# One level of Strassen's recursion in the first product of a squared-ReLU MLP, with the weight sums on POOL

## Chip, cores and metric

The kernel runs on one core of a Trainium2 chip. The metric is the device time of one execution in microseconds; before the change it was 2098.53 us, the median of three runs (2090.01 to 2098.53). In the profile PE is TensorE's matmuls, PEld its weight loads, DVE VectorE, ACT ScalarE, POOL GpSimd and SP the engine that issues the loads.

## What is computed

A trunk of two layers works on 640 tokens of 1024 features: 128 tokens of a prompt and 512 of a sample. Each layer has a token mixer (spatial gating in layer 0, RWKV-7 in layer 1) and an MLP; both are residual and behind an RMS norm that is modulated by a condition (adaLN). Only the MLP's line is touched:

```python
h = _rmsnorm(x, P['norm2_g'][l]) * (1 + sc2) + sh2
x = x + g2 * (jnp.square(jax.nn.relu(h @ P['mlp_w1'][l])) @ P['mlp_w2'][l])
```

`mlp_w1` is 1024 x 4096 and `mlp_w2` 4096 x 1024, in float32.

## The kernel before

Activations lie feature-major: a tile is 128 features by 640 tokens, and the 1024 features are 8 tiles. Products in float32 precision are made from float32r operands: each operand is split in a high and a low part (ScalarE casts, VectorE subtracts), and three products are summed, high by high, high by low and low by high. So one output tile of an MLP product takes 8 k-chunks x 3 parts x 2 token ranges = 48 matmuls, of 256 and of 384 columns in turn (`mmh`, L112 to L114; the halves HS are tokens 0 to 255 and 256 to 639, since a PSUM bank holds 512 float32 numbers of a partition). The sum of an output tile lies in one of three PSUM buffers (`fmps`).

`mlp` (L406 to L453) goes in four blocks (fb). In each block the first product gives 8 of the 32 hidden tiles, and the second product adds their share to the 8 output tiles. `fm` (L230) drives both: for each output tile it takes the 512 KB weight tile that has been loaded and split one group ahead (L82 to L89: a load on SP, a cast of 128x1024 on ScalarE at L88, a subtraction on VectorE at L89), runs the 48 matmuls and calls the evacuation. For the first product that is `ev1`: ReLU on ScalarE (L433), the square on VectorE (L435), and the split (L100, L101). For the second it is the residual sum on VectorE (L283). In the first block the first tiles are taken token half by token half (three tiles in layer 0, two in layer 1), since the second half's normalized activations are made (`enter`, L417) while PE works on the first half's. In layer 0 this is also where eight steps of the last adaLN projection run (`ada_steps`, L117, called by a hook after output tiles); PE takes about 1 us for one. Layer 0 takes the half of 256 tokens first, layer 1 that of 384.

Engines run their instructions in order, and a scheduler has put each engine's in an order by priority. The MLP of layer 0 runs from about 243 to 704 us of the profiled execution, that of layer 1 from about 1635 to 2093 us.

Of the kernel before, what the change touches and what calls it, by code (L numbers as in the profile page):

```python
# [7 lines left out]
F32 = mybir.dt.float32  # L8
# [20 lines left out]
def tile_trunk(ctx: ExitStack, tc: tile.TileContext, a: dict):  # L29
# [128 lines left out]
    class Norm:  # L158
# [5 lines left out]
        def add(self, k, r=(0, T)):  # L164
            for h, (t0, t1) in enumerate(HS):
                if r[0] <= t0 and t1 <= r[1]:
                    if self.acc[h] is None:
                        self.acc[h] = self.pool.tile([P, t1 - t0], F32, tag=f"acc{h}", name="acc")
                    self.gather(h, k == 0, X[k][:, t0:t1], self.pool.tile([P, 384], F32, tag="sq", name="sq")[:, :t1 - t0])
# [8 lines left out]
        # in two steps, with room for other products while the first one's result is worked on  # L178
# [49 lines left out]
    # groups: (tiles, order) - order of token halves when a group takes them one after the other, with its feature  # L228
    # tiles inside ("k": as inputs come) or one by one ("n": so that the first half is done early)
# [47 lines left out]
    # first half's statistics while the second half's products run  # L277
# [9 lines left out]
    def sgu(wp, norm):  # L287
        with ExitStack() as es:
# [8 lines left out]
            with ExitStack() as e2:  # L297
# [18 lines left out]
                # the first products follow their inputs, tile by tile  # L316
# [61 lines left out]
            up = Pool(es, "sguu", {"ah": 8, "al": 8})  # L378
# [24 lines left out]
    MB = (4, 3, 11)  # L403
    ST = ((3, 7), (2, 4))

    def mlp(wp, norm, l, first, last, hp=None, mp=None, pre=None):  # L406
        with ExitStack() as es:
            hp = hp or Pool(es, f"mlph{l}", {"ah": 8, "al": 8})
            sp = Pool(es, f"mlps{l}", {"ah": MB[2] if l else 11, "al": MB[2] if l else 11})
            mp = mp or Pool(es, f"mlpm{l}", {"r": 2, "q": 2})  # L410
            pre = pre or [wp.get(a["w1"][l, n]) for n in range(3)]
            n0 = len(pre)
            pp = Pool(es, f"pml{l}", {"f": 3}, PSUM)
            hs = [parts(hp) for _ in range(KT)]
            o0, o1 = map(int, first[1:])

            def enter(h):  # L417
                with urgent(h != o0):
                    bc = norm.rstd(h)
                    for k in range(KT):  # L420
                        fill(hs[k], norm.apply(k, bc, l, 1, h), HS[h])

            enter(o0)
            nn = Norm(npool)
            if l == 0:
                side.append(ada_steps(wp, 1, 0, 2))
            for fb in range(4):
                ss = {}

                def ev1(n, ps, rg):  # L430
                    m = rg[1] - rg[0]
                    r = mp.tile([P, T], F32, tag="r", name="relu")[:, :m]
                    act.activation(out=r, in_=ps, func=AF.Relu)  # L433
                    q = mp.tile([P, T], F32, tag="q", name="rsq")[:, :m]
                    vec.tensor_tensor(out=q, in0=r, in1=r, op=ALU.mult)  # L435
                    if n not in ss:
                        ss[n] = parts(sp)
                    fill(ss[n], q, rg)

                fm(wp, pp, "f", list(range(8)), lambda n: a["w1"][l, fb * 8 + n], hs, ev1,  # L440
                   [(n0, first)] + [1] * (8 - n0) if fb == 0 else None,
                   {(o0, ST[l][0]): lambda: norm.stats(o1), (o0, ST[l][1]): lambda: enter(o1)} if fb == 0 else {},
# [1286 lines left out]
```

## Time and profile before

| what | value |
|---|---|
| median of three runs | 2098.53 us |
| runs | 2090.01, 2098.53, 2098.53 us |
| span of the profiled execution | 2109.0 us |
| MLP of layer 0, about | 243 to 704 us |
| MLP of layer 1, about | 1635 to 2093 us |
| HBM traffic over the span | 123 GB/s |

The profiled execution's span is the time that its rows cover, 10.5 us above the median of the runs without the profiler. Rows of a timeline give an instruction's start, its duration and, in brackets, the idle time of its engine ahead of it with what ended that. Rows of a group give the count, then the sum of the durations in us and the mean in ns, then the idle time ahead of all of them. A row of a window gives the stretch in us, then busy time and count for PE, PEld, DVE, ACT and POOL, then the granted TensorE clock (1.00 is full speed), the DMA share and GB/s.

### The profile page before, as it was taken

What the parts mean: (1) busy time and instruction counts of PE and PEld (TensorE: products, weight loads), DVE (VectorE), ACT (ScalarE), POOL (GpSimd) and SP (SyncE); (2) the same over time, 40 slices, a digit from 0 to 9 for tenths busy, and PEclk for the clock granted to TensorE, in tenths of its full rate; (3) what the DMA queues carried; (4) which work ended last, traced back from release to release, by engine and by line L of the source; (5) the groups of instructions that cost most, each with busy time, mean ns of one, the idle gap of its engine ahead of it and who ended that gap; (6) DMA issues with size and microseconds to landing.
All of it is one profiled execution on the core that took longest, in us unless ns stands there. A gap on an engine that the chain in (4) does not pass through costs nothing.

```text
span 2109.0 us, 39157 instructions
## 1 busy us (share of the span) xinstructions
PE 1991.5 (94%) x15882; PEld 1739.6 (82%) x15882; DVE 1162.9 (55%) x2308; ACT 774.5 (37%) x1737; POOL 389.3 (18%) x689
## 2 busy tenths in 40 slices
PE   6999999999999789988869999999998999999997
PEld 5777889999999678877747766767787999999996
DVE  5435643333333796766786577787658533333334
ACT  5323531312222255444524444554434522222231
POOL 0000000000000200477551465465201000000000
PEclk9999999999999889987869879998799999999998
DMA  8777352222222033554655444552242222222221
GB/s 286 265 266 233 105 184 80 71 81 70 80 71 75 36 96 121 171 151 129 186 159 175 143 131 148 166 160 80 71 130 76 67 74 75 76 74 77 73 67 51
DMA packets 124438, 254.58 MB, mean 121 GB/s; under 512 B 24417, under 2 KB 63969, under 8 KB 124129
## 3 DMA queue, kind: packets, MB, share of 16 engines
q1 hardware_dynamic: 123824, 251.62, 37.3%
q8 instruction: 125, 2.05, 0.4%
q14 instruction: 57, 0.46, 0.1%
q10 hardware_dynamic: 432, 0.46, 0.1%
HBM read 214.67 MB, written 45.22 MB: 123 GB/s over the span
## 4 chain that ended last, share of the span: by engine, by line
PE 85%; DVE 6%; POOL 3%; ACT 2%; issue 2%; DMA 1%; SPq 0%; DVEq 0%; POOLq 0%; ACTq 0%
PE fmps L114 47%; PE zps L310 6%; PE p L910 4%; PE wops L1180 3%; PE vps L751 2%; PE za L1039 2%; PE za L1026 2%; PE sy L1053 2%; PE sy L1034 1%; PE rps L114 1%; PE trps L932 1%; PE adaps L1166 1%; PE adaps L122 1%; PE sy L1036 1%; PE tps L980 1%
## 5 line engine op out<-in xcount | busy, mean ns | idle before, releaser
L114 PE MATMUL fmps<-ahi,whi 128*128 128x256 f32 (+1 forms) x2272 | 534.6, 310 | 4.9 <-ACT ahi L100 3.1
L114 PE MATMUL fmps<-alo,whi 128*128 128x256 f32 (+1 forms) x2272 | 533.8, 309 | 1.3 <-DVE alo L101 1.3
L114 PE MATMUL fmps<-ahi,wlo 128*128 128x256 f32 (+1 forms) x2272 | 533.8, 309 | 0.0
L114 PEld LDWEIGHTS fmps<-ahi,whi 128*128 128x128 f32 x2272 | 414.4, 188 | 11.0 <-ACT ahi L100 6.3
L114 PEld LDWEIGHTS fmps<-alo,whi 128*128 128x128 f32 x2272 | 415.0, 188 | 2.1 <-DVE alo L101 1.8
L114 PEld LDWEIGHTS fmps<-ahi,wlo 128*128 128x128 f32 x2272 | 415.2, 188 | 1.0 <-issue 0.8
L88 ACT CAST whi<-wraw 128x1024 fp32r<-128x1024 f32 x174 | 182.6, 1050 | 632.6 <-PE fmps L114 538.2
L89 DVE TENSOR_TENSOR wlo<-wraw,whi 128x1024 fp32r<-128x1024 f32 x174 | 214.4, 1233 | 276.2 <-ACT whi L88 276.1
L283 DVE SCALAR_TENSOR_TENSOR x<-fmps,mod,x 128x128 f32<-128x128 f32 (+2 forms) x153 | 74.5, 527 | 305.4 <-PE fmps L114 305.4
L491 POOL TENSOR_TENSOR xx<-h 128x254 f32<-128x254 f32 (+1 forms) x16 | 12.1, 754 | 721.2 <-DVE h L210 706.1
L841 POOL TENSOR_TENSOR inv<-inv 128x220 f32<-128x220 f32 (+29 forms) x217 | 100.7, 464 | 114.4 <-DVE inv L834 57.7
L910 PE MATMUL p<-W,IT 128*128 128x256 f32 x320 | 109.6, 453 | 10.0 <-DVE B L925 5.9
L843 POOL TENSOR_TENSOR inv<-inv 128x220 f32<-128x220 f32 (+29 forms) x217 | 104.5, 482 | 16.9
L1042 ACT ACTIVATE RZ<-za 64x64 f32<-64x64 f32 x320 | 58.4, 214 | 66.7 <-PE za L1039 53.9
L1060 DVE TENSOR_TENSOR RZ<-sy,PC 64x64 f32<-64x64 f32 x256 | 49.4, 219 | 60.2 <-PE sy L1054 52.5
L101 DVE TENSOR_TENSOR alo<-rsq,ahi 128x640 fp32r<-128x640 f32 (+2 forms) x69 | 53.6, 776 | 45.6 <-ACT ahi L100 45.3
L100 ACT CAST ahi<-rsq 128x640 fp32r<-128x640 f32 (+2 forms) x69 | 47.5, 689 | 82.2 <-DVE rsq L435 81.8
L910 PEld LDWEIGHTS p<-W,IT 128*128 128x128 f32 x320 | 57.9, 211 | 22.9 <-DVE B L925 6.3
L1054 PE MATMUL sy<-RZ,B 128*64 128x64 f32 x640 | 72.6, 251 | 0.6 <-ACT RZ L1042 0.6
L1026 PEld LDWEIGHTS za<-RZ,W 128*64 128x64 f32 x640 | 43.5, 154 | 33.8 <-DVE RZ L1060 9.0
L1026 PE MATMUL za<-RZ,W 128*64 128x64 f32 x640 | 62.5, 254 | 8.4 <-DVE RZ L1080 5.9
L1036 PE MATMUL sy<-RZ,W 128*64 128x64 f32 x640 | 69.1, 249 | 0.0
(289 smaller groups left out, 3428.4 us busy)
## 6 DMA issues: line engine op xcount, KB each, us to landing
wraw<-w SPq DMA_DIRECT2D x126, 512.0 KB, 3.5
wraw<-ada SPq DMA_DIRECT2D x64, 512.0 KB, 4.9
W<-dKR SPq DMA_DIRECT2D x80, 256.0 KB, 3.5
adaw<-adac SPq DMA_DIRECT2D x32, 512.0 KB, 4.4
dKR<-zero SPq DMA_DIRECT2D x32, 320.0 KB, 6.3
dKR<-KR SPq DMA_DIRECT2D x32, 320.0 KB, 4.1
dIT<-IT SPq DMA_DIRECT2D x16, 640.0 KB, 3.3
IT<-dIT SPq DMA_DIRECT2D x80, 128.0 KB, 2.9
```

The costliest lines, as they stand in the source:

```text
L88: act.copy(hi[:, :n], r[:, :n])
L89: vec.tensor_tensor(out=lo[:, :n], in0=r[:, :n], in1=hi[:, :n], op=ALU.subtract)
L114: pe.matmul(ps[:, PS0 + t0:PS0 + t1], w, x[:, t0:t1], start=start, stop=stop)
L283: vec.scalar_tensor_tensor(out=X[n][:, t0:t1], in0=ps[:, t0 - r[0]:t1 - r[0]], scalar=mod[l][:, which, n, g:g + 1], in1=X[n][:, t0:t1], op ...
L310: pe.matmul(pss[i], x[:, i * P:(i + 1) * P], w[:, kq * 512:(kq + 1) * 512], start=(k == 0 and j == 0), stop=(k == KT - 1 and j == 2))
L841: eng.tensor_tensor(out=tv, in0=LA[:, s + 1:32, s:s + 1].to_broadcast([P, n, m]), in1=LX[:, s:s + 1, c0:c1].to_broadcast([P, n, m]), op=AL ...
L843: eng.tensor_tensor(out=LX[:, s + 1:32, c0:c1], in0=LX[:, s + 1:32, c0:c1], in1=tv, op=ALU.subtract)
L910: pe.matmul(ps[:, :, 2 * e:2 * e + 2].rearrange("p h s t -> p h (s t)"), IT[:, e], W[:, :, 2 * e:2 * e + 2].rearrange("p h s t -> p h (s t ...
L1026: pe.matmul(za[a0:a0 + 64, 0], W[:, h, 3 * e], RZ[:, ti, h, c], start=True, stop=True)
L1036: pe.matmul(sy[y0:y0 + 64, h], W[:, h, 1 + e], RZ[:, ti, h, c], start=h == 0, stop=False)
L1054: pe.matmul(sy[y0:y0 + 64, h], B[:, h, 3 * e], RZ[:, ti, h, c], start=False, stop=h == 1)
L1180: pe.matmul(ps, u, v, start=start and j == 0, stop=stop and j == 2)
```

## The change

The first product of an MLP is a product of a 2 x 2 block matrix of weights (two output tiles by two halves of the 1024 input features) with a 2 x 2 block matrix of activations (the two halves of the input features by two halves of 320 tokens). A *pair* of output tiles is now made by seven products of quarters instead of eight. Each of the seven has 4 k-chunks x 3 parts = 12 matmuls of 320 columns, so a pair has 84 matmuls of 320 columns where two tiles had 96 of 256 or 384. Their operands are sums of quarters:

- **Activations**, once in a layer (`combos`): the two quarters that are used plainly are copied or left in place, four sums of quarters are made and split. For each of four j that is an add of 640 on POOL and one on VectorE (L596, high part and low part of a tile back to one number), four combinations of 320 on VectorE (L600), a cast of 1280 on ScalarE (L562) and its low part on VectorE (L563).
- **Weights**, for each pair (`Pair.make`): four sums of 128x512 on POOL (L475 to L478), in place in the raw tiles but for the first, s1, which has a ring of two slots; then splits: one of 1024 and five of 512. The weights of a product are made two steps ahead, in a ring of three; five raw tiles are loaded ahead.
- **Results** (`pair`): the seven sums go through three PSUM banks A, B and C in the order of products 2, 1, 5, 6, 3, 7, 4. Products that belong to several quarters of the result are accumulated in one bank; ScalarE copies, VectorE adds, then one instruction does ReLU and square (L607), and the split follows as before.

The first four output tiles of each layer stay plain (`first_mm`, `first_out`; L613 to L630), 14 pairs follow. The second product is as before. Its order of blocks is the same too. The adaLN steps have moved from the first tiles into the second products of blocks 1 to 3. Scratch of the norm has smaller rings (squares 3 to 2, statistics 4 to 2 and others), the raw and split pools belong to the MLP alone, and the plain tiles' scratch (`ct`) shares the ring of s1.

```diff
+    ORD = ((2, "C", 512), (1, "A", 0), (5, "B", 0), (6, "A", 512), (3, "B", 0), (7, "A", 512), (4, "C", 0))
+    RAW = 5
...
+            tp = Pool(es, f"mq{l}", {"s": 2})
+            Th = [Pool(es, f"mh{l}{j}", {"t": 1}).tile([P, 2, 7, N2], F32R, "t", "th") for j in range(4)]
+            scr = Pool(es, f"mx{l}", {"s": 1})
...
+                def make(self, i):
+                    g = nc.gpsimd
+                    w = ring()
+                    a11, a12, a21, a22 = (x[:, c:c + 512] for x in self.t for c in (0, 512))
+                    h = [(w[0][:, c:c + 512], w[1][:, c:c + 512]) for c in (0, 512)]
+                    if i == 0:
+                        split_w(w, self.t[0])
+
+                        self.s1 = tp.tile([P, 512], F32, "s", "s1")
+                        g.tensor_tensor(out=self.s1, in0=a21, in1=a22, op=ALU.add)
+                        g.tensor_tensor(out=a21, in0=a11, in1=a21, op=ALU.subtract)
+                        g.tensor_tensor(out=a11, in0=a22, in1=a21, op=ALU.subtract)
+                        g.tensor_tensor(out=a12, in0=a12, in1=a11, op=ALU.subtract)
+                    elif i == 1:
+                        split_w(h[0], self.s1)
+                        split_w(h[1], a11)
+                    elif i == 2:
+                        split_w(h[0], a12)
+                        split_w(h[1], a21)
+                    else:
+                        split_w(h[0], a22)
+                    return w, 1 if i > 1 else 0
...
+            def combos():
+                for j in range(4):
+                    h, w = (y[:, cut[0][0]:cut[0][1]] for y in upper[j])
+                    act.copy(Th[j][:, 0, 0], h)
+                    vec.tensor_copy(Th[j][:, 1, 0], w)
+                for j in range(4):
+                    E = SC[:, 4 * (j % 2):4 * (j % 2) + 4]
+                    x = E.rearrange("p s t -> p (s t)")
+                    for m in range(2):
+                        h, w = row(j + 4 * m, 0, T)
+                        (vec if m else nc.gpsimd).tensor_tensor(out=x[:, T * m:T * m + T], in0=h, in1=w, op=ALU.add)
+
+                    for o, i0, i1, op in ((B22, B22, B12, ALU.subtract), (B12, B12, B11, ALU.subtract),
+                                          (B11, B22, B11, ALU.add), (B21, B21, B11, ALU.subtract)):
+                        vec.tensor_tensor(out=E[:, o], in0=E[:, i0], in1=E[:, i1], op=op)
+                    put((Th[j][:, 0, 3:7], Th[j][:, 1, 3:7]), E)
...
+            def relu2(x, n, r):
+
+                vec.scalar_tensor_tensor(out=x, in0=x, scalar=0.0, in1=x, op0=ALU.max, op1=ALU.mult)
...
+                for e, (i, c, o) in enumerate(ORD):
+                    if e % 2 == 0:
+                        need(k, e // 2, 2)
+                        w = made.pop((k, e // 2))
+                    for j in range(4):
+                        mm(ps(c), chunk(w, o // P + j), at(j, SLOT[i]), j == 0 and i in (2, 1, 5, 4), j == 3, skip_group_check=True)
+                    if i == 1:
+                        act.copy(x(0), ps("A"))
+                        vec.tensor_tensor(out=x(0), in0=x(0), in1=ps("C"), op=ALU.add)
+                        relu2(x(0), up, cut[0])
+                    elif i == 6:
+                        act.copy(x(1), ps("A"))
+                    elif i == 5:
+                        act.copy(x(3), ps("B"))
+                    elif i == 3:
+                        vec.tensor_tensor(out=x(1), in0=x(1), in1=ps("B"), op=ALU.add)
+                        relu2(x(1), up, cut[1])
...
+            for m in range(n0):
+                for k in range(4, KT):
+                    first_mm(fs[m], ws[m], k, o1)
+                first_out(m, fs[m], HS[o1])
+                need(m, m, 3)
+            combos()
+            for m in range(n0, 4):
+                need(m, m, 1 if m == 3 else 2)
+                w, ps = made.pop((m, m)), bank()
+                for h in (o0, o1):
+                    for k in range(KT):
+                        first_mm(ps, w, k, h)
+                for h in (o0, o1):
+                    first_out(m, ps, HS[h])
...
-    NP = {"sq": 3, "acc0": 1, "acc1": 1, "st": 4, "dg": 2, "nh": 4}
+    NP = {"sq": 2, "acc0": 1, "acc1": 1, "st": 2, "dg": 2, "nh": 2}
```

Two places show how instructions move. The first is ScalarE in layer 0's MLP, where the first tiles are done. `relu` and `ct` are the scratch of an evacuation, `fmps` a PSUM bank, `rsq` the square, `whi`/`shi` a weight's high part, `th` the activation operands of the seven products, `bs` the scratch in which the activation sums are made, `cs` that of a pair's results. Before, the three first tiles' second halves and the tiles that follow:

```order
L433 ACTIVATE relu_2538<-fmps_2262 128x384
L100 CAST ahi_2410<-rsq_2526 128x384
L100 CAST ahi_2426<-rsq_2540 128x384
L88 CAST whi_2554<-wraw_2552 128x1024
L433 ACTIVATE relu_2607<-fmps_2558 128x640
L88 CAST whi_2625<-wraw_2623 128x1024
L100 CAST ahi_2611<-rsq_2609 128x640
```

Now, from the second of the four j to the first result copy of the first pair:

```order
L562 CAST th_2181<-bs_2204 128x1280
L626 ACTIVATE ct_2277<-fmps_2559 128x256
L452 CAST shi_2622<-wraw_2219 128x512
L452 CAST shi_2661<-wraw_2219 128x512
L562 CAST th_2185<-bs_2204 128x1280
L562 CAST ahi_2610<-ct_2277 128x256
L562 CAST th_2189<-bs_2204 128x1280
L626 ACTIVATE ct_2277<-fmps_2559 128x384
L649 COPY cs_2618<-fmps_2621 128x320
```

The fourth tile's bank (`fmps_2559`) was emptied in one piece when the tile was done; now the second piece of it stands behind the four casts of 1280, and these wait for VectorE's combinations.

The second place is VectorE in layer 0 between second products. Before, while one first-product tile ends and the next begins:

```order
L89 TENSOR_TENSOR wlo<-wraw,whi 128x1024 x2
L435 TENSOR_TENSOR rsq<-relu 128x640
L101 TENSOR_TENSOR alo<-rsq,ahi 128x640
L89 TENSOR_TENSOR wlo<-wraw,whi 128x1024
L435 TENSOR_TENSOR rsq<-relu 128x640
```

Now, in one steady pair from the first result's sum to the last one (`wraw` and `s1` are the weight quarters and sums of the next pair):

```order
L650 TENSOR_TENSOR cs_3636<-cs_3636,fmps_3637 128x320
L607 SCALAR_TENSOR_TENSOR cs_3636<-cs_3636 128x320
L563 TENSOR_TENSOR alo_3676<-cs_3636,ahi_3675 128x320
L453 TENSOR_TENSOR slo_3712<-wraw_3402,shi_3711 128x1024
L657 TENSOR_TENSOR cs_3636<-cs_3636,fmps_3638 128x320
L607 SCALAR_TENSOR_TENSOR cs_3636<-cs_3636 128x320
L563 TENSOR_TENSOR alo_3676<-cs_3636,ahi_3675 128x320
L453 TENSOR_TENSOR slo_3756<-s1_3715,shi_3755 128x512
L661 TENSOR_TENSOR cs_3636<-cs_3636,fmps_3639 128x320
L453 TENSOR_TENSOR slo_3756<-wraw_3402,shi_3755 128x512
L607 SCALAR_TENSOR_TENSOR cs_3636<-cs_3636 128x320
L664 TENSOR_TENSOR cs_3636<-cs_3636,fmps_3637 128x320
```

Where a tile had one split, one square and one low part, a pair has 18 instructions, and a result's sum stands between splits of the next pair's weights.

More of the change, by code (lines that the diff above doesn't have):

```diff
@@ L400, in sgu, with __init__, load @@
         return norm2
-    MB = (4, 3, 11)
+    N2 = T // 2
+    ORD = ((2, "C", 512), (1, "A", 0), (5, "B", 0), (6, "A", 512), (3, "B", 0), (7, "A", 512), (4, "C", 0))
+    RAW = 5
     ST = ((3, 7), (2, 4))
-    def mlp(wp, norm, l, first, last, hp=None, mp=None, pre=None):
-        with ExitStack() as es:
[L408 to L412, printed above, removed]
-            pp = Pool(es, f"pml{l}", {"f": 3}, PSUM)
-            hs = [parts(hp) for _ in range(KT)]
-            o0, o1 = map(int, first[1:])
+    class Ada:
+        def __init__(self, sp):
+            self.tiles, self.sp = [], sp
+        def load(self, src, n=1024):
+            return self.tiles.pop(0)
@@ L420, in enter @@
                     for k in range(KT):
-                        fill(hs[k], norm.apply(k, bc, l, 1, h), HS[h])
-            enter(o0)
[L424 to L442, printed above, removed]
-                   pre if fb == 0 else None)
-                def ev2(n, ps, r):
-                    residual(l, 5, n, ps, r)
-                    if fb == 3:
-                        nn.add(n, r)
-                fm(wp, pp, "f", list(range(8)), lambda n: a["w2"][l, fb, n], [ss[n] for n in range(8)], ev2,
-                   [1] * 5 + [(3, last)] if fb == 3 else None, early(nn, int(last[-1])) if fb == 3 else {})
@@ new lines, in mlp, with mm @@
+            ss = {}
+            def relu2(x, n, r):
+                vec.scalar_tensor_tensor(out=x, in0=x, scalar=0.0, in1=x, op0=ALU.max, op1=ALU.mult)
+                if n not in ss:
+                    ss[n] = parts(sp)
+                put([y[:, r[0]:r[1]] for y in ss[n]], x)
+            def mm(ps, w, x, first, last, **kw):
+                for z, (u, v) in enumerate(((w[0], x[0]), (w[0], x[1]), (w[1], x[0]))):
+                    pe.matmul(ps, u, v, start=first and z == 0, stop=last and z == 2, **kw)
@@ new lines, in mlp, with first_mm, first_out @@
+            chunk = lambda w, k: (w[0][:, P * k:P * k + P], w[1][:, P * k:P * k + P])
+            bank = lambda: pp.tile([P, 1024], F32, "f", "fmps")
+            def first_mm(ps, w, k, h):
+                t0, t1 = HS[h]
+                mm(ps[:, PS0 + t0:PS0 + t1], chunk(w, k), row(k, t0, t1), k == 0, k == 7)
+            def first_out(n, ps, r):
+                c = tmps[n % 2][:, 0:r[1] - r[0]]
+                act.activation(out=c, in_=ps[:, PS0 + r[0]:PS0 + r[1]], func=AF.Relu)
+                vec.tensor_tensor(out=c, in0=c, in1=c, op=ALU.mult)
+                if n not in ss:
+                    ss[n] = parts(sp)
+                put([y[:, r[0]:r[1]] for y in ss[n]], c)
@@ new lines, in second_out, with second_mm @@
+            def second_out(b, n, ps, r):
+                residual(l, 5, n, ps[:, PS0 + r[0]:PS0 + r[1]], r)
+                if b == 3:
+                    nn.add(n, r)
+            def second_mm(ps, w, k, h):
+                for z, (wi, xi) in enumerate(((0, 0), (0, 1), (1, 0))):
+                    mmh(ps, chunk(w, k)[wi], ss[k][xi], k == 0 and z == 0, k == 7 and z == 2, h)
+            need(0, 0, 2)
+            enter(o0)
+            fs = [bank() for _ in range(n0)]
+            tmps = [tp.tile([P, 512], F32, "s", "ct") for _ in range(2)]
```

192 lines of the change are left out of this document (181 added, 11 removed).

## The prediction, as it was put on record

> **What bounds the kernel now.** I read the page first: busy shares, then the chain of waits, then the costliest groups.
>
> ```profile
> span 2109.0 us, 39157 instructions
> ...
> PE 1991.5 (94%) x15882; PEld 1739.6 (82%) x15882; DVE 1162.9 (55%) x2308; ACT 774.5 (37%) x1737; POOL 389.3 (18%) x689
> ...
> PE 85%; DVE 6%; POOL 3%; ACT 2%; issue 2%; DMA 1%; SPq 0%; DVEq 0%; POOLq 0%; ACTq 0%
> ...
> L114 PE MATMUL fmps<-ahi,whi 128*128 128x256 f32 (+1 forms) x2272 | 534.6, 310 | 4.9 <-ACT ahi L100 3.1
> ```
>
> TensorE is busy for 94% and carries 85% of the chain; the largest share of its work are the fmps matmuls of L114, which both MLPs and a few smaller products issue. Then the table of windows for a stretch inside each MLP:
>
> ```profile
> 330.00:500.00 170.00, 170.00 (x1161) 170.00 (x1160) 57.03 (x71) 38.39 (x44) 0.00 (x0) 1.00 0.24 75
> 1700.00:1900.00 200.00, 200.00 (x1366) 200.00 (x1365) 68.53 (x85) 46.02 (x53) 0.00 (x0) 1.00 0.24 77
> ```
>
> In both, PE (second number) has no idle time, VectorE (57 of 170 us) and ScalarE (38) have much, and POOL has nothing to do at all. So inside an MLP less matmul time is less time, one for one, for as long as the other engines keep up. What a matmul costs there is the distance of neighbours in PE's timeline, since their rows overlap:
>
> ```profile
> 690.03 0.28 PE L114 MATMUL fmps<-ahi,whi 128*128 128x256 f32 x1
> 690.15 0.28 PE L114 MATMUL fmps<-alo,whi 128*128 128x256 f32 x1
> ...
> 695.07 0.34 PE L114 MATMUL fmps<-ahi,whi 128*128 128x384 f32 x1
> 695.25 0.34 PE L114 MATMUL fmps<-alo,whi 128*128 128x384 f32 x1
> ```
>
> 256 columns take 0.12 us, 384 between 0.17 and 0.18. The windows say it finer: matmuls of 256 and 384 columns take turns there, and 170.00 us for 1161 of them (or 200.00 for 1366) are 0.1464 each on the mean, so 384 columns take 0.173; and 320 columns, halfway between the two, take that mean, **0.1464 us**, if the time goes with the columns.
>
> **The change, part by part.** *Matmuls.* Two output tiles took 96 x 0.1464 = 14.05 us. A pair by seven products is 84 x 0.1464 = 12.30 us, 1.76 us less, and 1.76 us for each product. There are 14 pairs in a layer: 28 x 1.76 = **49.3 us** off PE. The second product and the first four tiles of a layer keep their matmuls.
>
> *VectorE and POOL in a steady pair.* Their prices come from the groups by shape, of the same operands where there are some:
>
> ```profile
> L89 DVE TENSOR_TENSOR wlo<-wraw,whi 128x1024 fp32r<-128x1024 f32 x174 | 214.4, 1233 | 276.2 <-ACT whi L88 276.1
> L435 DVE TENSOR_TENSOR rsq<-relu 128x640 f32<-128x640 f32 x59 | 48.3, 819 | 9.3 <-ACT relu L433 9.3
> L101 DVE TENSOR_TENSOR alo<-nh,ahi 128x384 fp32r<-128x384 f32 x24 | 12.7, 555 | 0.9 <-ACT ahi L100 0.8
> L101 DVE TENSOR_TENSOR alo<-nh,ahi 128x256 fp32r<-128x256 f32 x24 | 10.1, 423 | 12.3 <-ACT ahi L100 12.1
> L386 DVE SCALAR_TENSOR_TENSOR z<-mixps,bs,z 128x320 f32<-128x320 f32 x16 | 8.7, 548 | 7.4 <-PE mixps L384 7.3
> L1227 DVE TENSOR_TENSOR tmp<-tmp 128x512 fp32r<-128x512 f32 x6 | 4.1, 689 | 3.6 <-ACT tmp L1226 3.6
> L579 DVE COPY inv<-nkps 128x320 f32<-128x320 f32 x2 | 0.9, 487 | 0.3 <-PE nkps L557 0.3
> ```
> ```profile
> L1227 POOL TENSOR_TENSOR tmp<-tmp 128x512 fp32r<-128x512 f32 x5 | 6.4, 1276 | 71.8 <-ACT inv L1029 37.0 <-ACT tmp L1226 34.8
> ```
> ```profile
> 966.78 1.49 DVE L663 TENSOR_TENSOR IT<-IT,S 128x1280 f32<-128x1280 f32 x1
> 968.19 2.57 DVE L89 TENSOR_TENSOR wlo<-wraw,whi 128x1024 fp32r<-128x1024 f32 x1
> ...
> 997.02 1.22 DVE L89 TENSOR_TENSOR wlo<-wraw,whi 128x1024 fp32r<-128x1024 f32 x1
> 998.15 2.84 DVE L663 TENSOR_TENSOR IT<-IT,S 128x1280 f32<-128x1280 f32 x1
> ```
> ```profile
> 967.00 2.67 POOL L706 TENSOR_TENSOR k<-k,r 128x640 f32<-128x640 f32 x1 [6.25 <-issue]
> ...
> 997.24 2.41 POOL L706 TENSOR_TENSOR k<-k,r 128x640 f32<-128x640 f32 x1 [2.28 <-issue]
> ```
>
> Two things are read from the timelines of the last two fences. Back to back, VectorE starts the next instruction some 0.08 us before a row ends (a row of 1.49 is followed after 1.41, one of 1.22 after 1.13), so each counts with 0.08 less. And VectorE and POOL shut each other out: L663 alone takes 1.49, but begun at 998.15 while POOL's L706 runs (to 999.65) it takes 2.84, which is that remainder and its own time; POOL's L706 at 967.00 sits until L663 is through at 968.27 and then takes 1.40, and VectorE's L89 behind it takes 2.57 for 1.23. The Trainium skill, page "SBUF — State Buffer", section "SBUF: two separate sides", says that the port pair the two share is an exclusive lock held for a whole instruction, taken by a VectorE instruction with two SBUF inputs; the trace agrees (2.84 for 1.49), and by that page the four adds of a pair that read PSUM would stay out of the lock, so that a pair without any other overlap would take 12.7 instead of the 14.3 below, and the far end of a block's loss would be 1.6 instead of 8 us.
>
> A pair then gives VectorE one split of 1024 (1.14 at a stroke), five of 512 (5 x 0.60), four adds and four low parts of 320 (8 x 0.40, between the rows of 256 and 384), and four squares of 320 (4 x 0.47): **9.2 us** of 12.30. POOL's four sums are 4 x 1.28 = 5.1. Together 14.3 if they never overlapped: more than PE's 12.30. But they need not stand in each other's way. Walked through by these prices, VectorE waits for product 3 (between about 6.9 and 8.9 us of a pair), where two POOL sums fit, and the other two fall into its dense stretch and delay it by 2.6 us; the products that wait for it have 1.2 to 3 us of slack (three PSUM banks, weights two steps ahead), and of a block's 16 POOL sums six are done during the second product before it. ScalarE, with 0.62 for a cast of 512 (1.05 for 1024), stays near 6.5 us of 12.30. I take 1 us for each of the 6 whole blocks, **6 us**, between 0 (all hidden) and 4 x 2 = 8 us a block (14.3 − 12.30 for each pair).
>
> *The first pair of layer 0.* Here the new work has the least cover: before the first pair's third product (number 5) VectorE has to make the sums of the activation quarters. The rows that set the clock of this place:
>
> ```profile
> 254.89 2.77 PE L122 MATMUL adaps<-wraw,cs 128*32 128x512 f32 x20
> 257.63 0.62 PE L114 MATMUL fmps<-ahi,whi 128*128 128x384 f32 x2
> ```
> ```profile
> 255.28 1.94 DVE L210 TENSOR_TENSOR nh<-x,ssps 128x384 f32<-128x384 f32 x4
> ```
>
> VectorE begins the second half's entry at 255.28, PE its first matmul at 257.63. From there PE has 72 x 0.173 = 12.5 us for the three plain tiles' second halves, 7.03 for the fourth tile and 3.5 for products 2 and 1, and 0.7 us of waiting for the fourth tile's low part: it wants product 5 at 281.4. VectorE has, up to the last low part that this product reads, 62 instructions by the order: 22 of 384 (0.47), 5 of 256 (0.34), 4 copies (0.40) and 16 combinations (0.40) of 320, 4 adds of 640 (0.74), 4 low parts of 1280 (1.41), 5 splits of 512 (0.60) and 2 of 1024 (1.14): 33.9 us, to 289.2. So the lag is 7.8 us with POOL out of the way; POOL's sums in that stretch, four of 640 (1.40) and six of 512 (1.28), are 13.3 us more if each of them shuts VectorE out whole, 21 in all. I take **14 us**: VectorE is the one that never rests here, but waits for ScalarE's casts of 1280 leave POOL some room. The product's other condition lies in the same queue: it takes the bank of the fourth tile, which ScalarE empties (L626) only behind those casts.
>
> *The first pair of layer 1.* There the two preloaded tiles come first, so PE's cover is two plain tiles.
>
> ```profile
> 1655.07 0.42 DVE L101 TENSOR_TENSOR alo<-nh,ahi 128x256 fp32r<-128x256 f32 x1
> ...
> 1660.90 0.79 DVE L435 TENSOR_TENSOR rsq<-relu 128x256 f32<-128x256 f32 x2 [2.52 <-ACT relu L433]
> ```
>
> Entry ends at 1655.5. PE is through with the two tiles' second halves at about 1660; with two tiles (14.1) and two products (3.5) it wants product 5 at 1677.6. VectorE, up to the fourth tile's evacuation, still has 7 instructions of 384, 7 of 256, 15 of 320, 2 of 640, 4 of 1280 and 2 splits: 21.1 us, or 25.3 with three POOL sums of 1.40. Only then is the slot free in which the first pair's s1 is put, since it shares a ring of two with the plain tiles' scratch; the sum (1.28), the cast (0.62) and the split (0.69) follow, so the weights of product 5 are there at 1679.2 to 1683.4, and those of 6 and 3 wait for three more POOL sums. Lag 4 to 12 us, **10 us** taken, nearer the end with the lock.
>
> *PE after a long wait.* These rows of the timeline are from the start of layer 1's MLP:
>
> ```profile
> 1634.96 0.92 PE L189 MATMUL ssps<-ones,acc 128*128 128x1 f32 x4 [3.00 <-DVE acc L176]
> ...
> 1640.30 0.52 PE L114 MATMUL fmps<-alo,w1s 128*128 128x384 f32 x1
> 1640.62 0.84 PE L114 MATMUL fmps<-ahi,w1s 128*128 128x384 f32 x2
> ```
>
> After 3.00 us of idle time matmuls of 384 columns come every 0.32 us instead of 0.173, from 1635.74 until 1641.58: 18 matmuls, 2.7 us lost. Both heads hold a wait that long: **5.4 us**. The Trainium skill, page "TensorE: Matmul & The Clock Gate", section "Part 1: The HAM clock gate (the "warmup" mystery)", gives half the clock after an idle window of about 3.4 us and the full one after as long a busy window; by that the loss would be 1.7 us for each wait and the sum 2 us lower, and the trace has the slow stretch longer, 5.8 us.
>
> *The rest.* The adaLN steps that filled PE's 2.77 us at 254.89 move to later second products, where PE is never idle: **2.7 us**. Weight loads stay the same number of 512 KB, ahead by the same five or so tiles: nothing, as the DMA share of 0.24 in the MLP windows has room. The shorter rings of the norm's scratch: nothing, at most the 2.77 us of that row.
>
> Sum: −49.3 + 6 + 14 + 10 + 5.4 + 2.7 = **−11.2 us**. The profiled execution's own span is 2109.0, 10.5 above the median of the runs, 2098.53; the terms are differences, so I put them on the median: **2087 us**. Half a per cent, 10.5 us, is about what a measurement of this kernel can tell from no change.
>
> **The rivals.** (1) *Heads and blocks better hidden.* The order's walk is too strict about the lock: lags of 7.8 and 4, no loss in the blocks, one cold start. −49.3 + 11.8 + 2.7 + 2.7 = −32, 2066 us. For it speaks that POOL had no queue in the MLPs and can use VectorE's gaps; against it the two rows where a single POOL operation cost VectorE its whole length.
>
> (2) *The shared port becomes the bound in every pair* (slower). It decides where VectorE's 9.2 and POOL's 5.1 no longer overlap: a pair takes 14.3 instead of 14.05, so nothing of the 49.3 is left (+7 over 28 pairs), and the heads are at their far ends, 21 + 12, with 8 us of cold starts and adaLN steps: +48, 2146 us. For it: POOL's rows that double against VectorE. Against it: VectorE's wait for product 3 in each pair, and the second products, in which VectorE catches up.
>
> (3) *The heads eat most of it.* The pairs run as forecast, but at each head the casts, low parts and POOL sums go strictly one after the other, and each hand-over costs its row's full length: 27 us each instead of 14 and 10. −49.3 + 54 + 5.4 + 2.7 + 6 = +19, 2117 us.
>
> **How the numbers follow.** Forecast 0.48, between 2077 and 2099; rival 1 0.22; rival 2 0.13; rival 3 0.17. The range 2062 to 2125 takes in the forecast, rivals 1 and 3 and leaves out rival 2 and a little on the near side. Faster by over 0.5% (below 2088): rival 1 and a little over half of the forecast, 0.48. Slower by over 0.5% (above 2109): rival 2 and most of rival 3, 0.25. The same: 0.27. The forecast lies at the edge between faster and the same.
>
> **What would show it.** Right: in a window of steady pairs PE at 100% with 12.3 us a pair; PE idle of 10 to 20 us ahead of the first product 5 of layer 0, released by ScalarE's L626 or a low part of 1280, and some 10 us in layer 1 released by weights behind s1; matmuls of 320 at twice their interval after it; POOL rows of 512 longer than 1.28 where VectorE is dense. Wrong: PE idle of over 1 us in every pair with a DVE or ACT releaser (rival 2), heads that are twice or half as long (3 and 1), or 320 columns at another interval than 0.146, each 0.01 of which is 2352 x 0.01 = 24 us.

## The result, and the profile after

The changed kernel takes 2110.94 us (median of 14 runs, 2098.86 to 2122.6) beside 2095.67 us for the kernel before (14 runs, 2083.4 to 2105.56): 1.0088 times as long, 95% interval 1.0064 to 1.0111. It is slower, by 15 us going by the medians and by 18 going by the ratio; 11 us less had been forecast.

The page of the changed kernel, its span and its busy line:

```profile
span 2120.8 us, 39445 instructions
...
PE 1955.6 (92%) x15546; PEld 1696.3 (80%) x15546; DVE 1372.7 (65%) x2706; ACT 853.2 (40%) x1983; POOL 570.6 (27%) x809
```

PE works 36 us less (1991.5 before) and the span is 11.8 us longer. VectorE works 210 us more, POOL 181 us more. To compare stages I cut each profile at the MLPs: from a matmul of the first half's norm to the last matmul of the second product. The part between the two MLPs, which the change leaves alone, took 926.3 us in the profile of before, 928.5 after, and between 903 and 924 in the experiments, at granted clocks of 0.87 to 0.89. So one profile's span says little about differences of 10 us. I compare the two MLP stages, from one profile of each kernel, and whole times only with their intervals. The windows of the two stages, before:

```profile
238.43:708.66 470.23, 468.85 (x3177) 458.70 (x3176) 182.97 (x269) 134.93 (x198) 1.31 (x4) 1.00 0.27 91
1634.96:2092.55 457.59, 456.55 (x3086) 455.37 (x3086) 175.43 (x248) 129.99 (x185) 0.00 (x0) 0.99 0.21 67
sum 927.82, PE 925.40 PEld 914.07 DVE 358.40 ACT 264.92 POOL 1.31; mean PE 462.70 PEld 457.04 DVE 179.20 ACT 132.46 POOL 0.66
```

And after:

```profile
239.71:718.54 478.83, 452.10 (x3009) 438.40 (x3008) 286.17 (x464) 170.12 (x316) 85.79 (x61) 0.97 0.27 88
1647.00:2106.58 459.58, 439.26 (x2918) 433.53 (x2918) 280.35 (x449) 169.21 (x307) 94.40 (x60) 0.98 0.21 68
sum 938.41, PE 891.36 PEld 871.93 DVE 566.52 ACT 339.33 POOL 180.19; mean PE 445.68 PEld 435.96 DVE 283.26 ACT 169.66 POOL 90.10
```

Layer 0 is 8.6 us longer and layer 1 2.0. PE is busy 34 us less, but where its busy time filled the stages before (925 of 928), there are now 47 us of idle time, and the granted clock, 1.00 and 0.99 before, is 0.97 and 0.98. What PE waited for in layer 0, then in layer 1, from the table of waits after (total, times, longest):

```profile
PE fmps L615 <- ACT ct L626: 17.8, 1, 17.8
PE fmps L615 <- ACT ahi L562: 4.1, 2, 2.7
PE fmps L615 <- ACT cs L649: 2.4, 6, 0.6
PE fmps L615 <- DVE cs L661: 2.0, 3, 0.7
...
PE fmps L615 <- ACT ct L626: 8.9, 1, 8.9
...
PE fmps L615 <- ACT cs L649: 5.0, 1, 5.0
PE fmps L615 <- DVE cs L661: 3.6, 3, 1.2
```

Two heads, then, and small waits in every block. The releaser named for the long one is ScalarE's emptying of a bank, but what stands ahead of that on ScalarE waits for VectorE. VectorE's timeline after, in that wait (285.4 to 303.3):

```profile
281.27 2.58 DVE L563 TENSOR_TENSOR th<-bs,th 128x1280 fp32r<-128x1280 f32 x1
283.77 1.78 DVE L453 TENSOR_TENSOR slo<-s,shi 128x512 fp32r<-128x512 f32 x1
285.69 1.53 DVE L453 TENSOR_TENSOR slo<-wraw,shi 128x512 fp32r<-128x512 f32 x1
287.15 1.81 DVE L600 TENSOR_TENSOR bs<-bs 128x320 f32<-128x320 f32 x1
288.88 1.88 DVE L596 TENSOR_TENSOR bs<-th 128x640 f32<-128x640 f32 x1
290.69 1.75 DVE L453 TENSOR_TENSOR slo<-wraw,shi 128x512 fp32r<-128x512 f32 x1
292.37 0.48 DVE L600 TENSOR_TENSOR bs<-bs 128x320 f32<-128x320 f32 x1
292.77 1.48 DVE L563 TENSOR_TENSOR th<-bs,th 128x1280 fp32r<-128x1280 f32 x1
...
302.85 1.49 DVE L563 TENSOR_TENSOR th<-bs,th 128x1280 fp32r<-128x1280 f32 x1 [0.44 <-ACT th L562]
```

There is hardly a gap in it, and as long as POOL runs (its next rows) the same work takes about two to four times its own time: a split of 512 takes 1.5 to 1.8 us for 0.68, a combination 1.81 for 0.48, a low part of 1280 2.58 for 1.48. At 292.37, while POOL rests, the old durations are back. From 281.27 to 292.37 VectorE does six instructions in 11.1 us that come to about 5 us by their own durations; the six sums that POOL does from 281.08 on come to 7.8 us by theirs (1.28 for 512 and 1.40 for 640, before the change), so most of their length is taken from VectorE here. POOL's timeline beside it:

```profile
282.58 2.42 POOL L477 TENSOR_TENSOR wraw<-wraw 128x512 f32<-128x512 f32 x1
285.08 1.59 POOL L478 TENSOR_TENSOR wraw<-wraw 128x512 f32<-128x512 f32 x1
286.64 1.97 POOL L596 TENSOR_TENSOR bs<-ahi,alo 128x640 f32<-128x640 f32 x1
288.58 1.51 POOL L475 TENSOR_TENSOR s<-wraw 128x512 f32<-128x512 f32 x1
290.16 1.73 POOL L476 TENSOR_TENSOR wraw<-wraw 128x512 f32<-128x512 f32 x1
294.33 1.71 POOL L596 TENSOR_TENSOR bs<-ahi,alo 128x640 f32<-128x640 f32 x1 [2.43 <-DVE th L563]
```

The two take turns. VectorE's last combination of the activations runs at 300.99; behind it ScalarE makes the last cast and then empties the bank, and PE goes on at 303.26:

```profile
301.56 1.26 ACT L562 CAST th<-bs 128x1280 fp32r<-128x1280 f32 x1 [1.98 <-DVE bs L600]
302.72 0.48 ACT L626 ACTIVATE ct<-fmps 128x384 f32<-128x384 f32 x1
```

The low part that product 5 reads last ends only at 304.34. Product 5 takes 1.8 us and reads that part near its end, so a bank emptied ahead of the casts could have let it begin only a little earlier.

### The profile page after: what moved, and what is told of

It is laid out like the page before. It is cut to its first block, busy times and chain, and to the rows that moved or that the text cites. A ratio compares the mean times of both kernels' runs of the same rounds, so it can differ in the third digit from the quotient of the medians.

```text
span 2120.8 us, 39445 instructions
## 1 busy us (share of the span) xinstructions
PE 1955.6 (92%) x15546; PEld 1696.3 (80%) x15546; DVE 1372.7 (65%) x2706; ACT 853.2 (40%) x1983; POOL 570.6 (27%) x809
## 4 chain that ended last, share of the span: by engine, by line
PE 73%; DVE 13%; issue 5%; POOL 4%; ACT 4%; DMA 1%; SPq 0%; POOLq 0%; DVEq 0%; ACTq 0%
PE fmps L114 27%; PE fmps L615 9%; PE zps L311 5%; PE p L1202 4%; PE wops L1472 3%; PE vps L1043 2%; PE za L1331 2%; PE za L1318 2%; PE sy L1345 2%; DVE slo L453 2%; DVE cs L607 1%; PE sy L1326 1%; PE rps L114 1%; PE trps L1224 1%; PE adaps L1458 1%
## 5 line engine op out<-in xcount | busy, mean ns | idle before, releaser
L615 PE MATMUL fmps<-th,shi 128*128 128x320 f32 (+2 forms) x1144 | 258.6, 314 | 28.6 <-ACT ct L626 17.8
L615 PEld LDWEIGHTS fmps<-th,shi 128*128 128x128 f32 x1144 | 193.5, 190 | 36.7 <-ACT ct L626 18.1
L615 PE MATMUL fmps<-th,slo 128*128 128x320 f32 (+2 forms) x572 | 178.3, 312 | 0.2 <-DVE slo L453 0.2
L453 DVE TENSOR_TENSOR slo<-wraw,shi 128x1024 fp32r<-128x1024 f32 (+1 forms) x139 | 143.1, 1032 | 30.2 <-ACT shi L452 29.4
L114 PE MATMUL fmps<-ahi,shi 128*128 128x256 f32 (+1 forms) x640 | 151.7, 310 | 0.0
L114 PE MATMUL fmps<-ahi,slo 128*128 128x256 f32 (+1 forms) x640 | 150.9, 309 | 0.0
L114 PE MATMUL fmps<-alo,shi 128*128 128x256 f32 (+1 forms) x640 | 150.9, 309 | 0.0
L114 PE MATMUL fmps<-ahi,w1s 128*128 128x256 f32 (+1 forms) x768 | 148.3, 309 | 0.0
L475 POOL TENSOR_TENSOR s<-wraw 128x512 f32<-128x512 f32 x28 | 38.0, 1360 | 408.4 <-DMA wraw<-w 376.0
L615 PE MATMUL fmps<-th,w1s 128*128 128x320 f32 (+2 forms) x828 | 129.1, 313 | 12.9 <-ACT ct L626 8.9
L114 PEld LDWEIGHTS fmps<-ahi,w1s 128*128 128x128 f32 x768 | 127.2, 188 | 0.1
```

The source lines that it names most:

```text
L114: pe.matmul(ps[:, PS0 + t0:PS0 + t1], w, x[:, t0:t1], start=start, stop=stop)
L453: vec.tensor_tensor(out=dst[1], in0=x, in1=dst[0], op=ALU.subtract)
L615: pe.matmul(ps, u, v, start=first and z == 0, stop=last and z == 2, **kw)
```

## Experiments

The theory after this: each POOL sum costs VectorE its own length, VectorE is what PE waits for in the heads and in the blocks, and so the sums take back what the products save. The rivals: PE waits for the chain from POOL's result through its split, not for the port; ScalarE's order is at fault; or seven products save less than counted. A block below is one of the three whole blocks of four pairs in a layer; in layer 0 it took some 52.1 us after the change, once about 1 us for its adaLN step is taken off, and 49.2 is PE's rate. One block of each layer after the change, layer 0 with its adaLN step:

```profile
383.38:436.46 53.08, 51.52 (x346) 49.44 (x345) 43.48 (x68) 26.57 (x53) 13.76 (x10) 1.00 0.30 92
1781.72:1833.10 51.38, 50.07 (x338) 49.28 (x337) 42.10 (x66) 26.84 (x52) 15.68 (x10) 1.00 0.27 87
```

Ratios below are to the kernel before, timed beside each run.

**The weight sums left out.**

```diff
-                        self.s1 = tp.tile([P, 512], F32, "s", "s1")
-                        g.tensor_tensor(out=self.s1, in0=a21, in1=a22, op=ALU.add)
...
+                        self.s1 = a12
```

> The four sums of weight quarters on POOL are left out: the splits read the raw quarters, so the products are of other numbers; all products, splits and evacuations stay. Theory (the heads are long because each POOL sum shuts VectorE out for its whole length, six of them between 279.5 and 292 us; the blocks' small waits come from the same): the wait ahead of product 5 in layer 0 goes from 17.8 to about 10.5 us, layer 1 loses the wait of 4.96 us behind s1 and keeps that of 8.9, the blocks of four pairs go from 52.1 to about 50.5 us; in all some 20 us less, about 2091 us. Rival (VectorE's own work is the bound and POOL runs beside it): only the chain behind s1 in layer 1 goes, about 5 us less, 2106 us.

2074.94 us, ratio 0.9899 (0.9867 to 0.9932). The stages, whose row of sums is

```profile
sum 909.46, PE 880.00 PEld 866.92 DVE 509.90 ACT 340.94 POOL 20.88; mean PE 440.00 PEld 433.46 DVE 254.95 ACT 170.47 POOL 10.44
```

take 28.9 us less than after the change. The wait in layer 0 is 12.7 us, the wait behind s1 in layer 1 is gone, the other is 9.3, and the blocks are at 49.4 us without one wait. The fall is larger than the theory's 20, though the wait in layer 0 stayed above the 10.5 expected; the rival's 5 is out. VectorE's busy time falls by 57 us, though not one of its instructions was taken away: that is the time for which POOL had held it up. For the 112 weight sums it is 0.5 us each, and a sum takes 1.28 us or more on POOL. So over the whole stages the theory's "own length" is too much: VectorE loses it where it has no gaps, as in the head, and elsewhere less than half of it.

**The activation sums left out.**

```diff
-                        (vec if m else nc.gpsimd).tensor_tensor(out=x[:, T * m:T * m + T], in0=h, in1=w, op=ALU.add)
...
-                        vec.tensor_tensor(out=E[:, o], in0=E[:, i0], in1=E[:, i1], op=op)
```

> The activation sums are left out: no adds of 640 on POOL and VectorE (L596) and no combinations of 320 (L600); the four casts of 1280 and their low parts stay and read what lies in the scratch, so the operands of five products are other numbers. Theory (the heads are what eats the saving, and most of a head is these sums, 9.4 us of VectorE and 6 to 7 us of POOL in its way): the wait in layer 0 goes from 17.8 to about 2 us, the two in layer 1 from 13.9 together to about 6, the blocks stay at 52.1 us; some 26 us less with the slow clock behind the waits, about 2085 us. Rival (the wait is for the fourth tile's bank, which ScalarE empties behind its casts, whatever VectorE has to do): the casts are still there and the wait stays over 10 us; about 2103 us.

2085.19 us, ratio 0.9949 (0.9921 to 0.9977); the stages take 913.82 us, 24.6 less than after the change, with 26 expected. The waits ahead of the first pair's products fall from 17.8 to 6.3 us in layer 0, where about 2 was expected, and from 13.9 to 3.8 in layer 1, where about 6 was; the blocks stay at 52.2. The casts and ScalarE's order are still there and hold PE for 6.3 us and not for over 10, so the order is not the main cause.

**All sums on VectorE.**

```diff
-                    g = nc.gpsimd
+                    g = vec
...
-                        (vec if m else nc.gpsimd).tensor_tensor(out=x[:, T * m:T * m + T], in0=h, in1=w, op=ALU.add)
+                        vec.tensor_tensor(out=x[:, T * m:T * m + T], in0=h, in1=w, op=ALU.add)
```

> All sums that POOL made (four of 512 in a pair, four of 640 in a layer) are made by VectorE. Theory (POOL's place costs VectorE more than the sum itself does: 1.4 us of shut port against 0.60 for a sum of 512): the wait in layer 0 goes from 17.8 to about 10 us, layer 1 loses some 4, the blocks go from 52.1 to about 51 us although VectorE has 11.6 us of work in 12.3; about 15 us less, 2096 us. Rival (VectorE's work is the bound and POOL relieves it): heads 6 us longer, blocks 2 us longer each; about 2130 us.

2076.48 us, ratio 0.9897 (0.9857 to 0.9938): faster than before. The stages' row of sums:

```profile
sum 908.70, PE 883.70 PEld 870.01 DVE 571.61 ACT 339.48 POOL 0.23; mean PE 441.85 PEld 435.00 DVE 285.81 ACT 169.74 POOL 0.12
```

Beside the row of after: VectorE is busy for 571.61 us with all the sums on it, and for 566.52 when POOL made 180 us of them. POOL relieved it of 5 us. A block has no wait left, as its windows in this run show (layer 0 with one adaLN step, layer 1):

```profile
377.34:427.81 50.47, 50.47 (x345) 49.44 (x345) 42.21 (x78) 26.77 (x53) 0.00 (x0) 1.00 0.30 97
1746.92:1796.20 49.28, 49.28 (x337) 49.28 (x337) 40.70 (x76) 26.81 (x52) 0.00 (x0) 1.00 0.29 89
```

VectorE works 10.2 us of a pair's 12.3 (40.70 for four) and PE is never idle. The head of layer 0 keeps waits of 8.3, 2.0 and 1.2 us. The blocks fell further than the theory's 51 us, and the rival's 2130 us is out.

**Only the weight sums on VectorE**, the activation adds still on POOL (the first of the two lines above).

> Only the weight sums go to VectorE, the four activation adds of 640 in a layer stay on POOL. Theory (every POOL sum costs VectorE its length, and the weight sums are 10 of every 16 in the blocks and six of the ten in the head of layer 0): blocks 49.5 us as without any POOL sum, the waits in the head of layer 0 about 13 us; both MLP stages together about 912 us (908.7 with all sums on VectorE, 938.4 after the change). Rival (the activation adds are what makes the heads long): the heads stay at 17.8 and 14 us, about 925 us.

2084.77 us, ratio 0.9916 (0.9884 to 0.9949); stages 912.67 us, 912 expected. Waits of 10.1, 0.4 and 1.1 us in layer 0, blocks without a wait. The weight sums are most of it; the four activation adds that a layer has on POOL cost 4 us (912.67 − 908.70). Made by VectorE, the weight sums add 62 us to its busy time (571.80 in this run, 509.90 without them); made by POOL they added 57. So VectorE's total is about the same either way, and the 26 us between the two kernels (938.41 and 912.67) come from where its delays fall, or from the chain behind POOL's results. The next run takes that chain away.

**POOL's sums made for nobody.** The splits read raw quarters as in the first run, but POOL makes four sums for each pair into a scratch that is never read.

```diff
+                        for _ in range(4):
+                            g.tensor_tensor(out=self.s1, in0=a21, in1=a22, op=ALU.add)
+                        self.s1 = a12
```

> The splits read the raw quarters as in the run without weight sums, so the products are of other numbers, but POOL still makes four sums of 512 for each pair, into a scratch that nobody reads. Theory (it is the port that POOL takes from VectorE, whatever becomes of the result): the blocks are back at 51.5 to 52 us and the wait in layer 0 at 16 to 18 us; both MLP stages together about 930 us. Rival (it is the chain from POOL's result to the split that makes PE wait): nobody waits for POOL here, so the blocks stay at 49.5 us and the stages at the 909.5 us of the run without sums.

2105.88 us, ratio 1.0038 (1.0008 to 1.0068), stages 931.12 us: 21.7 of the 28.9 us are back, though no weight sum is waited for. A block of each layer, the first with its adaLN step:

```profile
385.94:438.26 52.32, 51.43 (x346) 49.47 (x345) 41.56 (x68) 26.77 (x53) 12.81 (x8) 1.00 0.30 94
1771.69:1821.46 49.77, 49.55 (x338) 49.28 (x338) 39.45 (x66) 26.82 (x52) 12.92 (x8) 1.00 0.28 89
```

In layer 0 that is 51.3 us without the step, near the theory's number, with waits of 0.3 to 0.6 us for the same instructions as after the change. In layer 1 it is 49.8, where the rival had 49.5: most of what a block lost there is gone. So for layer 1's blocks the theory is not shown. After the change ScalarE's cast of a sum begins there at 1806.91, just behind POOL's row for that sum (it ends at 1806.88), and VectorE waits for the cast, so the chain may have a share. But in this run the four sums of a pair also stand together right behind the loads, and may fall at a better place; the two are not told apart. In the head the run is less clean: the wait is 20.7 us, but an activation add on POOL stands behind eight sums that nobody needs, and VectorE waits 5.3 us for it.

**POOL's memsets in their place.**

```diff
+                        for _ in range(8):
+                            g.memset(self.s1, 0.0)
+                        self.s1 = a12
```

> As the last one, but POOL's instructions are eight memsets of 512 for each pair into that scratch: POOL writes and reads nothing. Theory (the lock is one between two instructions that both read SBUF on that port, as the Trainium skill has it on its page SBUF - State Buffer): VectorE is not held up, the blocks stay at 49.5 us and the stages at about 909.5 us. Rival (any POOL instruction holds VectorE up): blocks over 50.5 us, stages over 920 us.

2075.58 us, ratio 0.9885 (0.9845 to 0.9925), stages 911.92 us. POOL and VectorE at the head of layer 0, with the sums for nobody (POOL, then VectorE):

```profile
279.20 15.43 POOL L476 TENSOR_TENSOR s<-wraw 128x512 f32<-128x512 f32 x8 [8.99 <-DVE alo L562]
```
```profile
282.17 5.06 DVE L562 TENSOR_TENSOR th<-bs,th 128x1280 fp32r<-128x1280 f32 x2
```

and with the memsets:

```profile
280.57 4.62 POOL L476 MEMSET s<- 128x512 f32 x8 [8.98 <-DVE alo L562]
```
```profile
283.12 2.89 DVE L562 TENSOR_TENSOR th<-bs,th 128x1280 fp32r<-128x1280 f32 x2 [0.47 <-ACT th L561]
```

Two low parts of 1280 take 5.06 us beside sums and 2.89 beside memsets, which is their own time. The Trainium skill, page "SBUF — State Buffer", section "SBUF: two separate sides", says that a VectorE instruction with two SBUF inputs meets the lock only against a GpSimd instruction that reads SBUF; these rows agree. In the blocks this run tells nothing, as the memsets wait for no load and ran ahead of them.

**The squares on ScalarE.** Sums as in the changed kernel, ReLU and square moved.

```diff
-                vec.scalar_tensor_tensor(out=x, in0=x, scalar=0.0, in1=x, op0=ALU.max, op1=ALU.mult)
+                act.activation(out=x, in_=x, func=AF.Relu)
+                act.activation(out=x, in_=x, func=AF.Square)
```

> ReLU and square of the first product go to ScalarE (two instructions for VectorE's L607, and Square for L627), which has 6.5 of 12.3 us of work in a pair. Theory (VectorE is what PE waits for): VectorE has 1.9 us less in a pair and some 3.5 us less in a head; the blocks go from 52.1 to about 50.7 us, the heads lose 3 to 4 us each; about 14 us less, 2097 us. Rival (ScalarE's copies of the banks are what PE waits for in the blocks, as the releaser L649 says): ScalarE with 9.7 us in a pair is later with them, the blocks stay or get longer; 2111 us or more.

2088.23 us, ratio 0.9946 (0.9918 to 0.9974); stages 920.89 us, 17.5 less than after the change with 14 expected. The wait in layer 0 goes from 17.8 to 13.5 us, blocks from 52.1 to 51.0. ScalarE's stages go from 339 to 426 us of busy time and the blocks get shorter all the same, so the waits put down to ScalarE's copies were in the main VectorE's.

**A third slot in the ring of s1.**

```diff
-            tp = Pool(es, f"mq{l}", {"s": 2})
+            tp = Pool(es, f"mq{l}", {"s": 3})
```

> The changed kernel with a third slot in the ring that s1 shares with the plain tiles' scratch, so that in layer 1 the first pair's weight sums need not wait for the fourth tile's evacuation. Theory (POOL's sums cost VectorE their length wherever they stand, and VectorE is what the head waits for): the wait of 4.96 us behind s1 in layer 1 goes, but the sums now run while VectorE makes the activation sums, and the wait of 8.9 us ahead of it grows by 3 to 6 us; layer 1's stage within 2 us of 459.6. Rival (the shared slot is the cause of that wait): the wait goes and nothing comes instead; layer 1's stage at about 453 us.

2114.18 us, ratio 1.0054 (1.0023 to 1.0085), stages 936.72, layer 1 at 460.0 us. The waits in layer 1 now:

```profile
PE fmps L615 <- ACT ct L626: 14.4, 1, 14.4
PE fmps L615 <- DVE cs L661: 3.4, 3, 1.1
PE fmps L615 <- DVE th L563: 2.9, 2, 2.6
```

The wait of 5.0 us for L649 is gone and that for L626 has grown from 8.9 to 14.4: the sums come earlier and take the same time from VectorE. The slot was where the wait stood, not what caused it.

**No sums at all.** The edits of the first two runs together.

> Neither activation sums nor weight sums, on any engine: the splits read raw quarters and the casts of 1280 read the scratch, so the products are of other numbers; products, splits, casts and evacuations stay. Theory (49.3 us of PE time are really saved, and the sums are what takes them back): the blocks at 49.5 us, the wait in layer 0 under 2 us, those in layer 1 under 5; both MLP stages together about 888 us (927.8 before, 938.4 after the change). Rival (what the seven products bring is less, because splits, casts and copies alone already hold PE up): over 900 us.

2055.84 us, ratio 0.9790 (0.9751 to 0.9829); the stages:

```profile
sum 883.31, PE 876.41 PEld 864.06 DVE 481.87 ACT 339.75 POOL 0.23; mean PE 438.21 PEld 432.03 DVE 240.94 ACT 169.87 POOL 0.12
```

That is 44.5 us less than before, 888 expected and 883.3 measured. The long waits are gone from both heads. PE is busy for 49.0 us less than before (925.40 and 876.41), so the seven products save what was counted, and of the changed kernel's 938.41 us the weight sums take 28.9 (938.41 − 909.46) and the activation sums 26.2 (909.46 − 883.31); taken out in the other order they are 30.5 and 24.6. The same sums on VectorE alone take 25.4 (908.70 − 883.31).

**Towards a better version.** Sums on VectorE and squares on ScalarE:

> Both edits that helped together: all sums on VectorE, and ReLU and square of the first product on ScalarE. Theory (without POOL's lock the blocks are at PE's rate already, and only VectorE's work in the heads is left to wait for): the blocks stay at 49.5 us, the wait in layer 0 goes from 11.5 us in all to about 8, the two in layer 1 from 8 to about 6; both MLP stages together some 5 us under the 908.7 us of the kernel with the sums on VectorE; ratio to before about 0.988. Rival (ScalarE's copies of the banks come late once it has 9.7 us of work in a pair): the blocks go over 50 us and the sum of the stages does not fall.

2073.8 us, ratio 0.9867 (0.9834 to 0.9901), stages 901.62 us, 7.1 less than with the sums alone on VectorE. Blocks at PE's rate, waits of 8.2 us in layer 0 and 3.1, 2.3 and 0.4 in layer 1. With the third slot as well:

> Sums on VectorE, squares on ScalarE, and the third slot. Theory: without POOL the chain behind s1 is shorter, so only the 2.3 us wait behind it in layer 1 can go: layer 1's stage at 439 to 441 us (441.3 without the slot), layer 0 at 460. Rival (the sums made early delay the activation sums on VectorE by their own 0.6 us each): no change or 1 to 2 us longer.

2070.89 us, ratio 0.9853 (0.9800 to 0.9906), stages 898.55 us; in layer 1 the 5.6 us ahead of L627 (the bank's emptying, one line further down here) is the one wait left in the head, and layer 1 takes 440.0 us, as the theory had it. This version beats both kernels, by about 1.5 and 2.3%; that the slot itself adds something is within the intervals.

## Why the prediction was wrong

The time lies inside the stated range, but on the other side of no change, and near a rival's number rather than the forecast's. The step that failed is the cover that the text gave POOL's sums: it counted them as mostly hidden behind VectorE's gaps in the blocks and partly in the heads. For the two MLP stages, which became 10.6 us longer, the terms come to:

| term | forecast, us | measured, us |
|---|---|---|
| matmuls saved | −49.3 | −49.0 |
| blocks | 6 | about 14 |
| waits in the heads | 14 + 10 | 17.8 + 16.1 |
| slow clock, more than before | 5.4 | 8 to 9 (estimate) |
| adaLN steps | 2.7 | 2.7 |
| sum | −11.2 | about +10 |

**The saving of 49.3 us** was right. With no sums in the way the stages are 44.5 us shorter and PE's busy time 49.0; the rest are waits, 2.7 us of them at the place that the adaLN steps had filled.

**The blocks, 6 us in all,** is the term that was furthest off for its size. They cost about 14: 53.0 to 53.1 us against 50.5 three times in layer 0 (with the adaLN step in both), and 51.4 to 51.6 against 49.3 three times in layer 1. The text put two of a pair's POOL sums into VectorE's wait for product 3 and gave the other two slack to fall into. That wait is not in the traces: none of the 28 additions that take product 3's result (L657) waits for PE, neither after the change nor with all sums on VectorE. The gap that VectorE has there lies ahead of the split of 1024, which waits for ScalarE's cast: 6.0 us in a block of layer 0 without the weight sums. POOL's sums of a pair follow the loads and the split of 1024, and in layer 0 they fall beside that split and the square. The rows

```profile
404.53 2.32 DVE L453 TENSOR_TENSOR slo<-wraw,shi 128x1024 fp32r<-128x1024 f32 x1
406.77 0.47 DVE L657 TENSOR_TENSOR cs<-cs,fmps 128x320 f32<-128x320 f32 x1
407.28 1.29 DVE L607 SCALAR_TENSOR_TENSOR cs<-cs 128x320 f32<-128x320 f32 x1
```
```profile
404.34 1.43 POOL L476 TENSOR_TENSOR wraw<-wraw 128x512 f32<-128x512 f32 x1
406.93 1.30 POOL L477 TENSOR_TENSOR wraw<-wraw 128x512 f32<-128x512 f32 x1 [1.16 <-DVE slo L453]
```

from the timelines of VectorE and POOL after show it: the split takes 2.32 us for 1.22 and the square 1.29 for 0.49. Why the slack of 1.2 to 3 us did not take up the rest is not shown. How much of the loss is the port's and how much the chain's is open in layer 1, as the run with sums for nobody left it.

**The heads, 14 and 10 us,** had the right mechanism and too small a size. PE wanted product 5 at 285.4, not 281.4, and VectorE began the second half's entry at 258.46, not 255.28; VectorE was through at 304.3, a little beyond the far end of 302 that the text had worked out (289.2 and 13.3 us of POOL). The wait was 17.8 us. In layer 1 the waits in the first pair were 8.9, 0.2 and 5.0 us, and 2.0 us more came in the plain tiles. There the text's own rows give a lag of only 1.6 to 5.8 us for product 5; the rest of its 4 to 12 was for three more sums and was not worked out. The text took values in the middle because ScalarE's casts "leave POOL some room"; in the timeline they left hardly any. In layer 0's head the sum at the full price of the lock, which the text had as an end of the range, was about right. In the blocks it was not: the full price was 8 us a block, and a block lost 2.1 to 2.6.

**PE's slow clock, 5.4 us,** was sized too small. The wait of 17.8 us was followed by matmuls of 320 columns at 0.265 us until 308.2, some 2.2 us lost. But there were more such stretches, one of them below. By the distances of neighbouring matmuls, which is an estimate, the stages lost 8 to 9 us more to them than before the change.

**The adaLN steps, 2.7 us.** Right: PE's wait at that place is 2.67 us.

**The rivals.** The third, at 2117 us, came nearest, but with heads of 27 us each and blocks as in the forecast; what happened is shared about evenly between weight sums, in heads and blocks, and activation sums, in the heads alone. The second had the right mechanism at too high a price. None of the three saw that the remedy was to take POOL out, although the rows for it were there: VectorE's own sum of 512 is 0.60 us and POOL's 1.28, and where VectorE is dense POOL's length is VectorE's loss.

## What to carry to other kernels

A POOL sum beside a VectorE that works on two SBUF inputs is no help where VectorE has no gaps: count its whole length against VectorE there, and move it only if that is less than VectorE's own time for it. Even over whole stages the 112 weight sums cost VectorE about as much on POOL (57 us) as made by itself (62). When work on PE is traded for work on other engines, walk the place where that work has the least cover (here the first pair), and look at whose rows have grown there before believing the releaser that the waits name. When one queue has no gaps, giving the place where a wait stands another slot only moves the wait.

## What the runs showed of the hardware

PE slowed down after a shorter wait than the forecast had reckoned with. Layer 0's first matmuls after the change follow a wait of 1.41 us:

```profile
245.87 0.38 PE L615 MATMUL fmps<-ahi,shi 128*128 128x256 f32 x1 [1.41 <-ACT ahi L562]
...
248.31 0.41 PE L615 MATMUL fmps<-ahi,shi 128*128 128x256 f32 x1
248.52 0.41 PE L615 MATMUL fmps<-alo,shi 128*128 128x256 f32 x1
```

They come every 0.21 us instead of 0.12, until about 250.1; the granted clock is 0.50 between 248 and 250 us. The Trainium skill, page "TensorE: Matmul & The Clock Gate", section "Part 1: The HAM clock gate (the "warmup" mystery)", asks for an idle window of about 3.4 us before the clock is halved; here 1.41 us was enough. But it is not the length of the wait alone: in the run with no sums at all the same matmuls follow a wait of 1.41 us too (they begin at 248.59), as sparse at first, and from 250 to 252 us they come every 0.12 us at a granted clock of 1.00. What decides it stays open.

A memset on POOL does not hold VectorE up and a sum does: the rows are above. An addition that reads PSUM passes beside a POOL sum. Four of the 28 additions of L657 begin under one and take 0.47 to 0.48 us like the rest, where 20 squares (L607) that begin under one take 1.28 to 1.59 for 0.49. One of the four, with POOL's row:

```profile
1803.94 0.47 DVE L657 TENSOR_TENSOR cs<-cs,fmps 128x320 f32<-128x320 f32 x1
```
```profile
1803.01 2.16 POOL L476 TENSOR_TENSOR wraw<-wraw 128x512 f32<-128x512 f32 x1
```
